# A delta-rule layer worked in pairs of heads: corrected queries as transposes, and the values' share in one bank

## The chip, the cores and the metric

The kernel runs on one core of a Trainium2 chip. The metric is the device time of one execution in microseconds (us). Engines are named as the profile names them: PE is TensorE's matmul stream and PEld its weight loads, DVE is VectorE, ACT is ScalarE, POOL is GpSimd and SP the queue that starts most DMAs. Each engine works through its instructions in the order in which they stand, so an instruction that waits holds up what is behind it on the same engine.

## The reference

A trunk of four layers on a sequence of 1024 tokens with 1024 features, in float32. Layers 0 and 3 mix tokens with a short convolution, layer 1 with a diagonal state-space model, layer 2 with the RWKV-7 delta rule. After each mixer come a gated embedding and a LayerNorm. The change lies in layer 2, whose core is a recurrence over time, one 64 x 64 state per head, 16 heads:

```python
def _rwkv_step(state, inp):
    r_t, w_t, k_t, v_t, kk_t, a_t = inp
    sa = jnp.einsum("bhvk,bhk->bhv", state, -kk_t)
    state = (state * w_t[:, :, None, :] + sa[..., None] * (kk_t * a_t)[:, :, None, :]
             + v_t[..., None] * k_t[:, :, None, :])
    out = jnp.einsum("bhvk,bhk->bhv", state, r_t)
    return state, out
```

The kernel does not step through time. It cuts the sequence into chunks of 64 tokens, solves the coupling inside a chunk with a triangular inverse, and carries the state from chunk to chunk.

## The kernel before

The sequence is worked in two halves of 512 tokens (h = 0, 1). In a half, each of eight units m is a block of 128 features, that is a pair of heads, with eight chunks. The chunks stand in pairs: w = 0 or 1 says which of a pair, and so which 64 of the 128 partitions a chunk's rows take. Of every unit the kernel does these things, each a generator that is pulled between the others:

- The projections `sp` (k and r of the next units, `mm3`, lines 326 to 328) are long products of 512 columns on PE. Each weight is split into a high and a low part, with three products per k-tile. They are the filling between everything else.
- `use_k` and `use_r` build the rows of keys and queries (`kb`, `ra`) and, by transposes, `ant`.
- `prep` multiplies `kb` with `ra` to scores `s` (line 1995), masks them on DVE into `sca` (line 1999), copies others into `scr` (ACT, line 2001), gathers the blocks `dg` and transposes them into `mi` (DVE, line 2012), multiplies the values `uv` with `sca` (`wps`, line 2021), copies that into the rows of `uv` (line 2025), and transposes `kb` into two tiles `kbt`.
- `tsolve` inverts the triangle on DVE in 11 steps.
- `join` completes the inverse `tt` (products `zp`, `tp`, lines 2090 and 2098) and applies it: to `ant`, giving `at` (line 2113), to `ant` again with the operands exchanged, giving `a2` (line 2119), which is the corrected part of the queries and is copied into `ra` (line 2124), and to `kbt` through `at`, giving `gt` (line 2134), copied into `gbd` (line 2138).
- `seq` forms `p` = inverse times values (line 2164), `pd` (line 2179), walks the eight chunks (`pd<-state,gbd` on PE, line 2185, and the state's update on DVE, line 2186), multiplies the queries with the states (line 2194) and adds the scores times values (line 2201) to the output.
- `tail` and `back` normalize and transpose the output.

A unit's `prep` is followed by the `join` of the unit before it, whose `seq` then runs beside the next unit's projections.

What sets the order: a scheduler takes the instructions by priority (`join`, `prep`, `seq` and `tsolve` are raised) and hands out buffers from pools as they come free; the order on each engine comes out of that. The pools that matter here are `aux`, two PSUM banks, through which all of these small products and transposes go, and `a1`, 16 tiles of 128 x 512. In the first half, eight of these 16 hold the low parts of the inputs of the k projection (`xs1`). Of each unit, `a1` holds one of the two `uv` and the two `scr` in both halves, and in the second half also `ant`, two `kbt`, `tt` and `at`. A tile of `a1` is free again when the last instruction that uses it is done: for `uv` and `scr` that is the last product of line 2201 in that unit's `seq`.

Of the kernel before, what the change touches and what calls it, by code (L numbers as in the profile page):

```python
# [8 lines left out]
F32 = mybir.dt.float32  # L9
# [6 lines left out]
P = 128  # L16
# [122 lines left out]
def setup_consts(S):  # L139
    nc, A = S.nc, S.A  # L140
    S.ident = S.const.tile([P, P], F32, tag="ident", name="ident")
    make_identity(nc, S.ident)
    S.mean_w = S.const.tile([P, P], F32, tag="mean_w", name="mean_w")
    nc.gpsimd.memset(S.mean_w, 1.0 / D)
# [1389 lines left out]
CH = 64  # L1534
# [394 lines left out]
def inner_setup(S, rg, T_):  # L1929
    nc = S.nc  # L1930
# [27 lines left out]
    def aux(nm):  # L1958
        return S.paux.tile([P, HT], F32, tag="aux", name=nm)
# [4 lines left out]
    zero = rg.tile([P, 2], F32, tag="zero", name="zero")  # L1964
    G.memset(zero, 0.0)
# [7 lines left out]
    def prep(m, h, R):  # L1973
# [42 lines left out]
        pss = [aux("wps"), aux("wps")]  # L2016
        for c in range(4):
            for hd in range(2):
                for w in range(2):
                    rb, rk = rows_b[w], rows_k[w]  # L2020
                    last = nc.tensor.matmul(pss[w][rb, c * P + hd * 64:c * P + hd * 64 + 64], sca[rk, w, c, hd, :],
                                            R.uv[w][rk, c, hd * 64:hd * 64 + 64], start=True, stop=True)
        for w in range(2):
            rb = rows_b[w]
            SC.copy(R.uv[w][rb].rearrange("p a b -> p (a b)"), pss[w][rb, :])
# [45 lines left out]
    def join(m, h, R):  # L2071
# [35 lines left out]
        with S.tc.issue_after(last.ins):  # L2107
# [7 lines left out]
            ps = [aux("a2"), aux("a2")]  # L2115
            for c2 in range(4):
                for hd in range(2):
                    for w in range(2):
                        nc.tensor.matmul(ps[w][heads[hd], c2 * CH:(c2 + 1) * CH], an[rows_b[w], c2, heads[hd]],
                                         tt[rows_b[w], 2 * c2 + hd, :], start=True, stop=True)  # L2120
        at = slot(S, ("a0", "a1")[h], "at").rearrange("p (c s) -> p c s", c=4)
        SC.copy(at.rearrange("p c s -> p (c s)"), pa)
        for w in range(2):
            SC.copy(r5[:, :, w, acol[w]], ps[w][:, 0:256].rearrange("p (c t) -> p c t", c=4))
# [11 lines left out]
        for w in range(2):  # L2136
            for hd in range(2):
                SC.copy(g5[heads[hd], :, w, heads[hd]], pg[w][heads[hd], 0:256].rearrange("p (c t) -> p c t", c=4))
        yield
# [3 lines left out]
    def seq(m, h, R, dST):  # L2143
# [13 lines left out]
        for ph in range(2):  # L2157
            p1 = S.pseq.tile([P, 2, 2, P], F32, tag="p1", name="p1", bufs=2)
            clear(p1[:, 0, 0, 0:2])
            for k in range(2):  # L2160
                for hd in range(2):
                    for w in range(2):
                        rb = rows_b[w]
                        nc.tensor.matmul(p1[rb, w, k, heads[hd]], R.tt[rb, 2 * (2 * ph + k) + hd, :],
                                         R.uv[w][rb, 2 * ph + k, heads[hd]], start=False, stop=False, skip_group_check=True)
# [127 lines left out]
```

## Time and profile before

| | us |
|---|---|
| median of 3 runs (lowest, highest) | 2805.72 (2804.64, 2808.44) |
| the profiled execution | 2808.62 |
| its span in the trace | 2806.6 |
| PE busy | 2709.2 (97%) |
| DVE busy | 1961.2 (70%) |
| ACT busy | 1215.7 (43%) |
| POOL busy | 649.2 (23%) |
| DMA queue 1, share of 16 engines | 38.9% |

The page of the profile gives busy times over the whole span. A stretch is read from the windows, a wait from the list of waits, and an order of events from the timeline. A small float32 product of this kernel leaves two matmul records in the trace, and a transpose leaves one. In the trace, layer 2's units run from about 1300 to about 2060 us.

### The profile page before, as it was taken

Reading aid. Unit: us, or ns where it says so; the run is one execution under the profiler, and the core shown is the slowest. Engines: PE = TensorE matmul, PEld = TensorE weight load, DVE = VectorE, ACT = ScalarE, POOL = GpSimd, SP = SyncE. Lnnn points to the kernel's source line nnn. Section 1 sums busy time; section 2 is a strip of 40 time slices with the busy share of each in tenths; the row PEclk is TensorE's granted clock in tenths of the full one; section 3 lists DMA queues with packets and bytes.
Section 4 is the critical chain, followed back from the end, with each engine's and each line's share of the span. In section 5 each row is a group of like instructions: output and inputs, shape, how many; then the busy total and the mean of one; then the engine's idle time right before and its main releaser. Section 6 shows DMA issues by size and latency. Waiting matters only on the chain.

```text
span 2806.6 us, 43661 instructions
## 1 busy us (share of the span) xinstructions
PE 2709.2 (97%) x16491; PEld 2171.2 (77%) x16491; DVE 1961.2 (70%) x3464; ACT 1215.7 (43%) x2147; POOL 649.2 (23%) x699
## 2 busy tenths in 40 slices
PE   8999999999999999999999889999999999999998
PEld 7877788777886888677787667777777877887887
DVE  6787765477657445897778766877756678877544
ACT  3333322242226223566566675666643343224332
POOL 0143421321115232202243200333332211111000
PEclk9999999999999999999999899999899999999999
DMA  5333321347785333464223245222334433324511
GB/s 170 99 98 98 88 83 57 89 139 207 212 240 165 98 99 88 139 222 139 72 80 102 74 153 175 73 87 74 105 117 142 132 120 106 102 71 133 171 64 38
DMA packets 463138, 331.22 MB, mean 118 GB/s; under 512 B 51496, under 2 KB 398928, under 8 KB 462928
## 3 DMA queue, kind: packets, MB, share of 16 engines
q1 hardware_dynamic: 462928, 328.43, 38.9%
q8 instruction: 130, 2.13, 0.3%
q14 instruction: 80, 0.66, 0.1%
HBM read 250.50 MB, written 77.33 MB: 117 GB/s over the span
## 4 chain that ended last, share of the span: by engine, by line
PE 75%; DVE 12%; issue 4%; ACT 4%; DMA 3%; POOL 1%; SPq 0%; DVEq 0%; ACTq 0%; POOLq 0%
PE op L327 4%; PE op L326 4%; PE op L328 4%; PE sp L327 3%; PE sp L326 3%; PE sp L328 3%; PE gp L328 3%; PE gp L327 3%; PE gp L326 3%; PE s L1995 2%; PE zp L326 2%; PE zp L327 2%; PE zp L328 2%; PE qa L507 2%; PE qa L506 2%
## 5 line engine op out<-in xcount | busy, mean ns | idle before, releaser
L298 ACT CAST wh<-wraw 128x1024 fp32r<-128x1024 f32 x255 | 267.3, 1049 | 527.1 <-PE gp L327 186.8
L299 DVE TENSOR_TENSOR wl<-wraw,wh 128x1024 fp32r<-128x1024 f32 x255 | 334.1, 1311 | 216.0 <-ACT wh L298 209.0
L905 POOL TENSOR_TENSOR ln_s<-ln_s,rp 128x512 f32<-128x512 f32 x42 | 60.4, 1438 | 208.6 <-DVE rp L901 208.5
L2062 DVE TENSOR_TENSOR tv<-ti,mi 128x128 f32<-128x128 f32 (+3 forms) x128 | 95.1, 743 | 2.2
L920 POOL TENSOR_TENSOR rp<-r_0h,r_0l 128x512 f32<-128x512 f32 x24 | 38.8, 1650 | 168.6 <-PE op L327 168.6
L328 PE MATMUL gp<-r_1h,wl 128*128 128x512 f32 x192 | 76.2, 397 | 0.4 <-DVE wl L299 0.4
L328 PE MATMUL gp<-r_0h,wl 128*128 128x512 f32 x192 | 76.5, 398 | 0.0
L326 PE MATMUL gp<-r_1h,wh 128*128 128x512 f32 x192 | 76.4, 398 | 0.0
L326 PE MATMUL gp<-r_0h,wh 128*128 128x512 f32 x192 | 76.0, 396 | 0.0
L327 PE MATMUL gp<-r_0l,wh 128*128 128x512 f32 x192 | 76.0, 396 | 0.0
L327 PE MATMUL gp<-r_1l,wh 128*128 128x512 f32 x192 | 75.3, 392 | 0.0
L1995 PE MATMUL s<-ra,kb 64*128 64x128 f32 x512 | 69.0, 295 | 2.2 <-ACT scr L2001 0.9
L1995 PEld LDWEIGHTS s<-ra,kb 64*128 64x128 f32 x512 | 58.2, 194 | 15.1 <-ACT scr L2001 5.2
L2186 DVE SCALAR_TENSOR_TENSOR state<-state,pc,pd 128x64 f32<-128x64 f32 x120 | 33.3, 278 | 42.9 <-PE pd L2185 41.6
L2170 ACT COPY uv<-p 64x256 f32<-64x256 f32 x128 | 46.9, 367 | 31.7 <-PE p L2194 26.2
L2185 PEld LDWEIGHTS pd<-state,gbd 128*128 128x128 f32 x240 | 42.5, 207 | 21.8 <-DVE state L2186 12.4
L327 PE MATMUL sp<-xs0l,wh 128*128 128x512 f32 x128 | 56.7, 443 | 1.9 <-DVE xs0l L195 1.9
L326 PE MATMUL sp<-xs3h,wh 128*128 128x512 f32 x128 | 52.6, 416 | 5.3 <-DVE sg L1663 5.3
L326 PE MATMUL sp<-xs0h,wh 128*128 128x512 f32 x128 | 56.6, 442 | 0.4 <-ACT xs0h L195 0.4
L2260 POOL TENSOR_TENSOR yt<-yt,bv 128x512 f32<-128x512 f32 x16 | 20.8, 1302 | 154.0 <-ACT yt L2259 110.5
L328 PE MATMUL sp<-xs0h,wl 128*128 128x512 f32 x128 | 55.7, 435 | 0.0
L195 ACT CAST r_0h<-r 128x512 fp32r<-128x512 f32 x32 | 19.9, 620 | 81.5 <-DVE r L406 39.4
(864 smaller groups left out, 8905.2 us busy)
## 6 DMA issues: line engine op xcount, KB each, us to landing
wraw<-in_conv_w_in_dram SPq DMA_DIRECT2D x84, 512.0 KB
wraw<-in_rwkv_w_rkvz_dram SPq DMA_DIRECT2D x64, 512.0 KB
wraw<-in_ple_gate_dram SPq DMA_DIRECT2D x56, 512.0 KB
wraw<-in_conv_w_out_dram SPq DMA_DIRECT2D x24, 512.0 KB
xt<-xd SPq DMA_DIRECT2D x48, 256.0 KB
wraw<-in_ssm_w_in_dram SPq DMA_DIRECT2D x21, 512.0 KB
xd<-rp SPq DMA_DIRECT2D x40, 256.0 KB
wraw<-in_rwkv_w_out_dram SPq DMA_DIRECT2D x16, 512.0 KB
```

What stands on the lines that cost most here:

```text
L298: nc.scalar.copy(wh, raw)
L299: nc.vector.tensor_tensor(wl, raw, f32(wh[:]), ALU.subtract)
L326: nc.tensor.matmul(ps, lh, xh, start=(n == 0), stop=False)
L327: nc.tensor.matmul(ps, lh, xl, start=False, stop=False)
L328: nc.tensor.matmul(ps, ll, xh, start=False, stop=(n == kt - 1))
L506: nc.tensor.matmul(ps, wh[:, k0 + k, :], xh, start=first and k == 0, stop=False, skip_group_check=True)
L507: nc.tensor.matmul(ps, wh[:, k0 + k, :], xl, start=False, stop=False, skip_group_check=True)
L905: nc.gpsimd.tensor_tensor(s, s, rs, ALU.add)
L1995: nc.tensor.matmul(pss[hd][:, c * P:(c + 1) * P], kb[rows, 2 * c + w, :], ra[rows, 2 * c + w, :], start=True, stop=True)
L2062: V.tensor_tensor(tv, ti[:, b:8, 4 * b:4 * b + 4].unsqueeze(2).to_broadcast([P, n, c, 4]), mi[:, 4 * b:4 * b + 4, 0:c].rearrange("p q c -> ...
L2170: SC.copy(R.uv[w][rows_b[w], 2 * ph:2 * ph + 2, :], p1s[ph][rows_b[w], w])
L2185: nc.tensor.matmul(col, R.g[:, c, :], sv[:, c, :], start=False, stop=True, skip_group_check=True)
```

## The change

Three edits.

1. In `join`, the second set of 16 products (`a2`, two banks) goes. Instead the tile `at`, once ACT has copied it, is turned by four transposes of 128 x 128 into one bank, and the two copies into `ra` read from there. These transposes and copies stand at the end of `join`, behind `gt` and its copies.
2. In `prep`, the 16 products of values and scores, which filled half of each of two banks, fill one bank. One copy of 128 x 512 moves it into a new tile `uvb` from the pool `a1`, where two copies of 64 x 512 moved it into the rows of the two `uv`. `seq` reads `uvb` in its first products.
3. The two columns of zeros with which `seq` clears its banks are written once among the constants at the program's start, ahead of the identity, and no longer in layer 2.

```diff
 def setup_consts(S):
+    S.zero = S.const.tile([P, 2], F32, tag="zero", name="zero")
+    nc.gpsimd.memset(S.zero, 0.0)
...
-        pss = [aux("wps"), aux("wps")]
+        pss = aux("wps")
...
-                    last = nc.tensor.matmul(pss[w][rb, c * P + hd * 64:c * P + hd * 64 + 64], sca[rk, w, c, hd, :],
+                    last = nc.tensor.matmul(pss[rb, c * P + hd * 64:c * P + hd * 64 + 64], sca[rk, w, c, hd, :],
                                             R.uv[w][rk, c, hd * 64:hd * 64 + 64], start=True, stop=True)
-        for w in range(2):
-            rb = rows_b[w]
-            SC.copy(R.uv[w][rb].rearrange("p a b -> p (a b)"), pss[w][rb, :])
+        R.uvb = slot(S, "a1", "uvb").rearrange("p (c s) -> p c s", c=4)
+        SC.copy(R.uvb.rearrange("p c s -> p (c s)"), pss)
...
-            ps = [aux("a2"), aux("a2")]
-            for c2 in range(4):
-                for hd in range(2):
-                    for w in range(2):
-                        nc.tensor.matmul(ps[w][heads[hd], c2 * CH:(c2 + 1) * CH], an[rows_b[w], c2, heads[hd]],
-                                         tt[rows_b[w], 2 * c2 + hd, :], start=True, stop=True)
         at = slot(S, ("a0", "a1")[h], "at").rearrange("p (c s) -> p c s", c=4)
         SC.copy(at.rearrange("p c s -> p (c s)"), pa)
-        for w in range(2):
-            SC.copy(r5[:, :, w, acol[w]], ps[w][:, 0:256].rearrange("p (c t) -> p c t", c=4))
         yield
...
+        ps = aux("a2")
+        for c2 in range(4):
+            nc.tensor.transpose(ps[:, c2 * P:(c2 + 1) * P], at[:, c2, :], S.ident)
+        p3 = ps.rearrange("p (c s) -> p c s", c=4)
+        for w in range(2):
+            SC.copy(r5[:, :, w, acol[w]], p3[:, :, acol[w]])
         yield
...
-                                         R.uv[w][rb, 2 * ph + k, heads[hd]], start=False, stop=False, skip_group_check=True)
+                                         R.uvb[rb, 2 * ph + k, heads[hd]], start=False, stop=False, skip_group_check=True)
```

The scheduler orders the program anew from the edits on; before layer 2's units and behind them the engines' orders are the same. PE in a `join` of the first half, before (`a_` is a bank of the second product, `p_` one of the two banks of inverse times values, `pss` belongs to the next unit's keys):

```order
L2113 MATMUL at<-ant,tt 64x64 x15
L2119 MATMUL a_12476<-tt,ant 64x64 x8
L2164 MATMUL p_12592<-uv,tt 64x64 x2
L2119 MATMUL a_12477<-tt,ant 64x64 x5
L2134 MATMUL gt<-kbt,at 64x64 x8
L2119 MATMUL a_12477<-tt,ant 64x64 x3
L2164 MATMUL p_12592<-uv,tt 64x64 x5
L2164 MATMUL p_12602<-uv,tt 64x64 x4
L2134 MATMUL gt<-kbt,at 64x64 x8
L2179 MATMUL pd<-uv,kbt 64x64 x2
```

The same place on PE in the changed kernel, where `a<-ident,at` are the four transposes:

```order
L2113 MATMUL at<-ant,tt 64x64 x15
L2162 MATMUL p_12549<-uvb,tt 64x64 x7
L2162 MATMUL p_12559<-uvb,tt 64x64 x4
L2126 MATMUL gt<-kbt,at 64x64 x16
L2177 MATMUL pd<-uv,kbt 64x64 x8
L2162 MATMUL p_12559<-uvb,tt 64x64 x3
L2133 MATMUL a_12470<-ident,at 128x128 x4
L330 MATMUL sp<-xs0h,wl 128x512
```

`gt` now stands in one piece, behind 11 products of `p`; the turned queries come last, with a projection directly behind them. The second place is PE in `prep` of the first half, before: `s_` are the four banks of scores of a unit, `p_12592<-uv,scr` and `p_12602` belong to the output of the unit before the last.

```order
L1995 MATMUL s_12835<-ra,kb 128x128 x4
L2185 MATMUL pd<-state,gbd_9913 128x64
L1995 MATMUL s_12858<-ra,kb 128x128 x4
L2185 MATMUL pd<-state,gbd_9913 128x64
L2201 MATMUL p_12592<-uv,scr 64x64 x3
L1995 MATMUL s_12859<-ra,kb 128x128 x4
L2201 MATMUL p_12592<-uv,scr 64x64
L2185 MATMUL pd<-state,gbd_9913 128x64
L2201 MATMUL p_12592<-uv,scr 64x64 x4
L327 MATMUL sp<-xs1l,wh 128x512
L2194 MATMUL p_12602<-sbd,ra 128x128 x4
```

And in the changed kernel (`p_12559<-uv,scr` are the last output products of that unit's `seq`; `s_12815` and `s_12816` are the third and fourth bank of scores):

```order
L2192 MATMUL p_12559<-sbd,ra 128x128 x4
L328 MATMUL sp<-xs1h,wh 128x512
L329 MATMUL sp<-xs1l,wh 128x512
L330 MATMUL sp<-xs1h,wl 128x512
L2151 MATMUL p_13035<-zero,ident 128x2
L328 MATMUL sp<-xs1h,wh 128x512
L329 MATMUL sp<-xs1l,wh 128x512
L2199 MATMUL p_12559<-uv,scr 64x64 x8
L330 MATMUL sp<-xs1h,wl 128x512
L328 MATMUL sp<-xs1h,wh 128x512
L1996 MATMUL s_12815<-ra,kb 128x128
L1996 MATMUL s_12816<-ra,kb 128x128
```

Before, all four banks of scores stand ahead of the last output products; now the third and fourth stand behind them. This is so in four units of the first half and in none of the second. Behind these scores the changed kernel has 12 projection products (16 in one of the four units), `wps` and the eight transposes of `kb` before the next `zp`.

## Rows read from the trace of the kernel before

**Rows 1.** The page: busy times, and the shares of the last chain.

```profile
PE 2709.2 (97%) x16491; PEld 2171.2 (77%) x16491; DVE 1961.2 (70%) x3464; ACT 1215.7 (43%) x2147; POOL 649.2 (23%) x699
...
PE 75%; DVE 12%; issue 4%; ACT 4%; DMA 3%; POOL 1%; SPq 0%; DVEq 0%; ACTq 0%; POOLq 0%
```

**Rows 2.** Windows: stretch, length; PE, PEld, DVE, ACT, POOL busy (instructions); PEclk, DMA share, GB/s.

```profile
1300.00:2060.00 760.00, 718.13 (x7368) 572.30 (x7367) 587.79 (x1234) 491.33 (x1049) 219.04 (x223) 0.94 0.33 101
...
1345.00:1545.00 200.00, 192.39 (x2375) 156.86 (x2375) 158.89 (x373) 131.81 (x304) 71.13 (x74) 0.95 0.29 88
```

**Rows 3.** PE's waits, 1290 to 2070 us (total, times, longest).

```profile
PE zp L2090 <- DVE t L2082: 6.5, 6, 3.0
...
PE pd L2185 <- DVE state L2186: 4.6, 6, 1.9
PE p L2201 <- ACT uv L2170: 4.1, 5, 1.5
PE gt L2134 <- ACT gbd L2138: 4.0, 13, 0.6
```

**Rows 4.** Timeline of PE in one join (start, duration, first to last end).

```profile
1457.88 0.93 PE L2113 MATMUL at<-ant,tt 64*64 64x64 f32 x26
...
1458.70 0.46 PE L2119 MATMUL a<-tt,ant 64*64 64x64 f32 x10
```

**Rows 5.** Timeline of PE around four transposes.

```profile
1449.79 0.39 PE L327 MATMUL sp<-xs0l,wh 128*128 128x512 f32 x1
1450.03 0.60 PE L2032 MATMUL kbtp<-ident,kb 128*128 128x128 f32 x4
1450.38 0.48 PE L328 MATMUL sp<-xs0h,wl 128*128 128x512 f32 x1
```

**Rows 6.** ACT's copies of lines 2122, 2138, 2025 (ns: min/median/max).

```profile
L2122 ACT COPY at<-at x16: 570/586/587, 1350.6 to 2048.6; 128x512 f32<-128x512 f32 x16
...
L2138 ACT COPY gbd<-gt x64: 361/367/370, 1352.6 to 2052.5; 64x256 f32<-64x256 f32 x64
...
L2025 ACT COPY uv<-wps x32: 564/582/588, 1312.5 to 2013.3; 64x512 f32<-64x512 f32 x32
```

**Rows 7.** Timeline from the last scores of a unit to `zp`.

```profile
1442.39 0.42 DVE L1999 TENSOR_TENSOR sca<-s,mask 128x256 f32<-128x256 f32 x1 [0.39 <-PE s L1995]
...
1442.85 0.82 ACT L2008 COPY dg<-sca 32x256 f32<-32x256 f32 x2 [0.43 <-DVE sca L1999]
...
1444.81 2.04 DVE L2012 STREAM_TRANSPOSE mi<-dg 128x1024 f32<-128x1024 f32 x1
...
1446.21 0.69 PE L2201 MATMUL p<-uv,scr 128*64 128x64 f32 x16
...
1446.98 0.65 ACT L2001 COPY scr<-s 128x256 f32<-128x256 f32 x2 [0.17 <-PE p L2201]
...
1447.92 1.15 PE L2021 MATMUL wps<-uv,sca 64*64 64x64 f32 x32
...
1451.58 1.12 DVE L2077 STREAM_TRANSPOSE tt<-ti 128x256 f32<-128x256 f32 x2
...
1452.56 0.40 DVE L2082 STREAM_TRANSPOSE t<-tt 128x256 f32<-128x256 f32 x1
...
1453.11 0.69 PE L2090 MATMUL zp<-t,m 32*32 32x32 f32 x32 [0.19 <-DVE t L2082]
```

**Rows 8.** Windows behind that join, and one near the start.

```profile
1460.00:1470.00 10.00, 9.79 (x124) 7.98 (x120) 6.81 (x17) 5.00 (x12) 3.88 (x4) 0.73 0.31 94
1470.00:1480.00 10.00, 10.00 (x81) 8.76 (x80) 8.47 (x23) 5.58 (x14) 1.42 (x3) 0.93 0.48 146
...
18.00:20.00 2.00, 2.00 (x6) 1.55 (x5) 1.41 (x2) 0.00 (x0) 0.00 (x0) 0.50 1.02 376
```

**Rows 9.** Timeline of PE at the program's start.

```profile
4.18 1.00 PE L211 MATMUL pxt<-ident,xraw 128*128 128x128 f32 x2 [4.18 <-DMA xraw<-in_x_dram]
...
8.05 6.26 PE L211 MATMUL pxt<-ident,xraw 128*128 128x128 f32 x29 [0.72 <-DMA xraw<-in_x_dram]
```

More of the change, by code (lines that the diff above doesn't have):

```diff
@@ L1962, in sq @@
         return S.pseq.tile([P, HT], F32, tag="sq", name=nm)
-    zero = rg.tile([P, 2], F32, tag="zero", name="zero")
-    G.memset(zero, 0.0)
+    zero = S.zero
     heads = [slice(hd * 64, hd * 64 + 64) for hd in range(2)]
```

## The prediction

> **What bounds the kernel now.** I read the page first: PE is busy for 97% of the span and has 75% of the chain that ended last; DVE has 12%, ACT 4% [rows 1]. Then the windows, because the change touches only layer 2's units: from 1300 to 2060 us PE is busy 718.1 of 760, and in the steady part of the first half 192.4 of 200 [rows 2]. So a unit is bound by PE's queue. DVE is busy 77% and ACT 65% there, which is not enough to set the end by throughput, but both release PE. The list of PE's waits shows where: `zp` on the end of DVE's solve 6.5 us, the chunk chain on the state 4.6, the output products on copied values 4.1, `gt` on the copies of `gbd` 4.0 [rows 3]. The reader is to see that no wait is long and that none stands for all units: PE has projections to do in between. Last, the granted clock: 0.94 over the 760 us [rows 2]. It has two levels, 2.4 and 1.2 GHz, so 0.94 means 12% of that time at the lower one, and 0.06 x 760 = 46 us of full-speed work not done.
>
> **The second product.** It goes in all 16 joins: 16 products each, 32 records. Two groups of such records, 26 in 0.93 us and 10 in 0.46 us, give (0.93 - 0.46) / 16 = 0.029 us for one more [rows 4], so 32 of them take 0.94 us. Four transposes take 0.35 us from their first start to the next product's start, and 0.60 to their own last end [rows 5]. A join so loses 0.59 us of PE by starts, 0.34 by ends. I take 0.50, nearer to the reading by starts, since the small products too are taken by starts. In the order of the change the last join of the first half has no projection beside it, so PE's time is not what counts there; 15 x 0.50 = 7.5 us off (bounds 5.1 and 8.8).
>
> **The waits of the join.** With two banks, before, the second half of `gt` had to wait until `gbd` was copied out: 4.0 us over 13 times [rows 3]. `gt` now stands in one piece, and this wait goes. Two come. `gt` needs the copy of `at`, 0.59 us [rows 6], with 11 products of `p` ahead of it, 22 x 0.029 = 0.64 us: I take 0.1 us per join for the hand-over. Behind `gt` are `pd`, the rest of `p` and the projections. The transposes need a bank, which comes free after two copies of `gbd`, 0.73 us [rows 6], covered by 8 products of `pd` and 3 of `p`, again 0.64 us: 0.15 us per join. Together 16 x 0.25 = 4.0, which is what went: 0, bounds -4 (full cover) and +4 (twice that). The copies into `ra` end later than before, but the first product that reads the queries stands only behind the chain's fifth step.
>
> **The values' share.** PE does the same 16 products. ACT does one copy in place of two of 0.58 us [rows 6], 9.3 us less over 16 units. ACT is busy 491 of 760 us [rows 2], so a third of its time is free and PE, not ACT, is the queue that is full: 0; if all of it were on the path it would be -9.3. The 16 products now write the two halves of one bank. If the halves had to take turns there, `wps` would take up to twice its 1.15 us [rows 7], 16 x 1.15 = 18 us more. The rows speak against it: `at` is written by two halves into one bank already, and its records are part of the 0.029 us above [rows 4]. The Trainium skill, "TensorEngine Tiling (Array Packing)", section "Gotcha 1: PSUM Pressure", says that different row tiles cannot use the same PSUM bank at the same time. By that rule the sum would end 18 us higher; the trace does not agree, as far as `at` shows it, and it is left as a rival with a small chance.
>
> **The zeros.** One tiny memset moves ahead of the identity. The first transpose waits for the input's DMA until 4.18 us [rows 9]: 0.
>
> **The tile `uvb`.** It is a fourth tile of `a1` per unit in the first half, where eight of 16 are taken. The last two score banks need `scr` tiles that come free with the last output products. Before, they were computed earlier and lay in the two banks until then: the copies waited for PE's output products to 1446.98 [rows 7]. Now the scores themselves stand behind these products in four units. From their end to `zp`, DVE and ACT need two masks at 0.42 us, `dg` 0.82, `mi` 2.04, `tt` 1.12, `t` 0.40 [rows 7]: 5.2 us, and hand-overs. PE has 12 projections at 0.24 us by starts [rows 5], `wps` 1.15 and eight transposes at 0.35 per four: 4.7 us. Before, PE waited 0.19 us here [rows 7]. I take 1 us per unit more, +4, and expect 3 of it back: projections that now stand inside the chunk chain cover some of the 8.7 us of waits there [rows 3]. Net +1, bounds -4 and +12 (3.0, the longest `zp` wait of the rows, in each of the four).
>
> **The sum.** -7.5 + 0 + 0 + 0 + 1 = -6.5 us. The profiled execution took 2808.6 us, 2.9 over the median of the runs; from it 2802.1, from the median 2799.2. I forecast 2799, with an own range of 2795 to 2802.
>
> **Rivals.**
>
> Clock, worse. Half clock follows joins: 0.73 and 0.93 in the two windows behind the one in the rows, 3.4 us of work lost in one fall [rows 8]. At the start 29 transposes in a row, then a pause, are followed by a window at 0.50 [rows 8, 9]. If transposes in place of products bring four more falls among 16 joins, +13.6 against -6.5 gives 2813: slower. The gain is gone from two more falls on (+6.8). Against it: four transposes last 0.35 us, and those of [rows 5] pass between projections of 0.39 and 0.48 us without a fall. The Trainium skill, "TensorE: Matmul & The Clock Gate", section "Part 4: PE-mode transpose", says that transposes do not count as PE work for the full clock; the trace's start agrees as far as it goes (0.50 after them).
>
> Clock, better. Projections now stand directly behind the turned queries, where there were only small products. Three falls fewer would be -10.2: 2789.
>
> `zp` waits. The solve's tail comes late in all four units by 3.0 us and none of it is given back: +12 - 7.5 = +4.5, 2810. For it: `zp`'s is the longest list of waits already. It decides where a unit's wait, less what comes back, is over 2 us.
>
> No gain. PE's shorter queue only waits longer for the state and the solve, as in the 42 us of 760 in which it is idle now: 2805. For it speaks that DVE's chain is 77% busy; against it, that idle time is spread thin.
>
> One bank costs: +18 - 6.5, 2817.
>
> **Chances.** My forecast 0.44, clock better 0.12, no gain 0.18, `zp` waits 0.11, clock worse 0.12, one bank 0.03. The range that holds 8 in 10 runs from 2788, a little under the better clock, to 2812, just short of the worse one. A measurement of this kernel can tell about 0.2%, 5.6 us, from no change, so faster means under 2800.1 and slower over 2811.3. Faster: the better clock and four fifths of the forecast, 0.47. Slower: the worse clock, one bank, a third of the `zp` case, 0.19. Same: the rest, 0.34.
>
> **What will show it.** Right: four records of `a<-ident,at` per join at about 0.35 us; PE's busy time from 1300 to 2060 down by 7 to 8 us; no wait of `gt` on `gbd`; `wps` at about 1.15 us in one bank. Waits of `zp` on `t` tell the slot case: over 10 us in total and it holds. PEclk over the units tells the clock: 0.94 for no change, under 0.93 or over 0.95 for a rival. I am wrong if the span changes by more than 3 us outside 1300 to 2060.

## The result, and the profile after

| | before, us | changed, us |
|---|---|---|
| median of 5 runs each (lowest, highest) | 2804.64 (2797.26, 2808.44) | 2790.42 (2786.80, 2792.86) |
| the profiled execution | 2808.62 | 2788.27 |
| its span | 2806.6 | 2786.4 |

The ratio is 0.995, 95% interval 0.9932 to 0.9969: the change is faster by 14.2 us. The forecast was 2799 in a range of 2788 to 2812. The side is right and the range holds the time, but the gain is about twice the one forecast (6.5), and the narrower range of the forecast alone, 2795 to 2802, does not hold it.

The page of the changed kernel: busy times, and the shares of the last chain.

```profile
PE 2681.5 (96%) x16043; PEld 2139.2 (77%) x16043; DVE 1962.9 (70%) x3464; ACT 1207.8 (43%) x2131; POOL 644.4 (23%) x699
...
PE 71%; DVE 15%; ACT 5%; issue 5%; DMA 3%; POOL 1%; SPq 0%; DVEq 0%; ACTq 0%; POOLq 0%
```

PE is busy for 27.7 us less than in [rows 1], at 448 records fewer: 16 joins lost 32 records each and got four. Its share of the chain fell, DVE's and ACT's rose.

The windows of the changed kernel (columns as in [rows 2]).

```profile
0.00:1300.00 1300.00, 1265.33 (x5898) 1009.70 (x5899) 878.48 (x1467) 465.53 (x698) 331.43 (x395) 0.99 0.45 134
1300.00:2060.00 760.00, 708.74 (x7015) 555.13 (x7015) 595.48 (x1253) 491.39 (x1049) 218.88 (x228) 0.94 0.33 102
2060.00:2786.40 726.40, 707.43 (x3134) 574.42 (x3132) 488.96 (x745) 250.91 (x384) 94.09 (x77) 0.99 0.36 110
1345.00:1545.00 200.00, 186.85 (x2215) 149.34 (x2214) 163.62 (x383) 133.44 (x305) 70.66 (x77) 0.94 0.31 95
```

From 1300 to 2060 us PE is busy 9.4 us less than in [rows 2], at the same granted clock of 0.94. This stretch is fixed while the units end earlier (their last `zp` starts at 2026.5 in place of 2044.0 us), so in the changed kernel it holds some 17 us of later work; what the change takes off PE is the 27.7 us of the whole span. The clock did not move, and what stands at half clock is looked at below.

PE's waits there, 1290 to 2070 us (total, times, longest).

```profile
PE zp L2090 <- DVE t L2082: 6.6, 6, 3.8
PE pd L2183 <- DVE state L2184: 5.9, 11, 1.8
PE zp L2090 <- DVE gn_s L1598: 4.7, 4, 1.4
PE a L2133 <- ACT gbd L2130: 3.5, 5, 1.4
PE s L1996 <- DVE kb L1741: 3.4, 5, 1.3
PE p L2199 <- ACT uv L2168: 2.7, 3, 1.5
```

Against [rows 3]: `gt` no longer waits for `gbd`; the transposes (`a`) wait for it instead, 3.5 us. The wait of `s` on `kb` grew, from 0.7 to 3.4. `zp` on `t` reads 6.6 as before, but the wait on `gn_s` has to be added to it, as the timeline of one of its four cases shows:

```profile
1377.83 0.39 DVE L2082 STREAM_TRANSPOSE t<-tt 128x256 f32<-128x256 f32 x1
1378.15 0.12 DVE L1598 TENSOR_TENSOR gn_s<-gn_s,rs_t 128x8 f32<-128x8 f32 x1
1378.37 0.69 PE L2090 MATMUL zp<-t,m 32*32 32x32 f32 x32 [1.42 <-DVE gn_s L1598]
```

`zp` reads `t`, which ends at 1378.22, and starts 0.15 us later; `gn_s`, the next instruction on DVE, ends 0.05 us behind `t`, and so the list names it. It is a wait for the solve like the others. All waits of `zp`, before and in the changed kernel (busy us, mean ns of one | idle before them and what ended it):

```profile
L2090 PE MATMUL zp<-t,m 32*32 32x32 f32 x512 | 11.1, 192 | 6.6 <-DVE t L2082 6.5
...
L2090 PE MATMUL zp<-t,m 32*32 32x32 f32 x512 | 11.5, 194 | 11.8 <-DVE t L2082 6.6 <-DVE gn_s L1598 4.7 <-DVE rs_t L1597 0.3
```

So `zp` waits 5.2 us more for the solve than before, and the prediction's sign for late scores, over 10 us in total, is met. In the four units with late scores it waits 1.4, 1.4, 1.4 and 0.3 us, 4.5 in all, where it waited 1.9 before. What that costs the experiments tell.

The timeline of PE in one join of the changed kernel (start, duration from the first start to the last end), which answers to [rows 4, 5].

```profile
1823.68 0.33 PE L2113 MATMUL at<-ant,tt 64*64 64x64 f32 x2
...
1824.08 1.03 PE L2113 MATMUL at<-ant,tt 64*64 64x64 f32 x29
1824.89 0.92 PE L2162 MATMUL p<-uvb,tt 64*64 64x64 f32 x22
1825.79 0.69 PE L2126 MATMUL gt<-kbt,at 64*64 64x64 f32 x32
1826.41 0.69 PE L2177 MATMUL pd<-uv,kbt 128*64 128x64 f32 x16
1827.03 0.44 PE L2162 MATMUL p<-uvb,tt 64*64 64x64 f32 x6
1827.40 0.65 PE L2133 MATMUL a<-ident,at 128*128 128x128 f32 x4
1827.81 0.48 PE L328 MATMUL sp<-xs1h,wh 128*128 128x512 f32 x1
```

From the first `at` to the projection behind the turned queries it is 4.13 us; the four transposes take 0.41 by starts and 0.65 to their own end. The 32 records of `gt` stand together and take 1826.41 - 1825.79 = 0.62 us, 0.019 each, where the forecast took 0.029 per record [rows 4].

What the small products of all 16 units take on PE, from 1300 to 2070 us, in the kernel before (busy us, mean ns of one | idle before them and what ended it; records that stand mixed count in both groups):

```profile
L2021 PE MATMUL wps<-uv,sca 64*64 64x64 f32 x512 | 29.9, 228 | 1.6 <-ACT scr L2001 1.6
L2119 PE MATMUL a<-tt,ant 64*64 64x64 f32 x512 | 29.1, 236 | 1.8 <-ACT at L2122 0.4
...
L2134 PE MATMUL gt<-kbt,at 64*64 64x64 f32 x512 | 22.4, 230 | 4.0 <-ACT gbd L2138 4.0
```

The same groups in the changed kernel:

```profile
L2022 PE MATMUL wps<-uv,sca 64*64 64x64 f32 x512 | 23.7, 235 | 2.5 <-DVE sca L2000 2.0 <-ACT scr L2002 0.3
L2126 PE MATMUL gt<-kbt,at 64*64 64x64 f32 x512 | 13.0, 241 | 0.7 <-ACT at L2116 0.3
L2133 PE MATMUL a<-ident,at 128*128 128x128 f32 x64 | 10.7, 286 | 3.6 <-ACT gbd L2130 3.5
```

The second product went from 29.1 to 10.7. But `gt` and `wps`, of which not one product went, fell too, by 9.4 and 6.2, at equal time of one record. They are busy for less because more of them run side by side: that is the reading on which the rest turns. The three falls add up to 34 us, more than PE's 27.7, because records that stand mixed count twice and other groups rose, for one the transposes `kbtp` of `kb`, from 18.2 to 21.8.

The values' share in one bank, on PE's timeline:

```profile
1372.54 1.22 PE L2022 MATMUL wps<-uv,sca 64*64 64x64 f32 x32 [0.15 <-ACT scr L2002]
1373.69 0.51 PE L328 MATMUL sp<-xs1h,wh 128*128 128x512 f32 x1
```

In the kernel before, the two banks of the first unit went one after the other, 16 records in 1.14 us each:

```profile
1309.70 1.14 PE L2021 MATMUL wps<-uv,sca 64*64 64x64 f32 x16
1310.77 0.50 PE L328 MATMUL sp<-xs1h,wl 128*128 128x512 f32 x1
1311.23 1.14 PE L2021 MATMUL wps<-uv,sca 64*64 64x64 f32 x16
```

Not all units before were like this: the one in [rows 7] had both banks free. And the copy behind the one bank, which answers to [rows 6] (ns: min/median/max):

```profile
L2025 ACT COPY uvb<-wps x16: 567/585/589, 1310.3 to 1998.3; 128x512 f32<-128x512 f32 x16
```

The 32 records written by two row halves into one bank last 1.22 us, against 1.15 in two banks in [rows 7], and one copy of 128 x 512 costs what each of the two copies of 64 x 512 cost. So two row halves in one bank cost at most 0.07 us, in 16 units about 1 us and not 18: that rival is out. The Trainium skill, "TensorEngine Tiling (Array Packing)", section "Gotcha 1: PSUM Pressure", says that different row tiles can't use the same bank at the same time; the trace does not agree, for two row halves that write different partitions of the bank.

### The profile page after: what moved, and what is told of

Read it like the earlier page. It is cut to its first block, busy times and chain, and to the rows that moved or that the text cites. A ratio compares the mean times of both kernels' runs of the same rounds, so it can differ in the third digit from the quotient of the medians.

```text
span 2786.4 us, 42742 instructions
## 1 busy us (share of the span) xinstructions
PE 2681.5 (96%) x16043; PEld 2139.2 (77%) x16043; DVE 1962.9 (70%) x3464; ACT 1207.8 (43%) x2131; POOL 644.4 (23%) x699
## 4 chain that ended last, share of the span: by engine, by line
PE 71%; DVE 15%; ACT 5%; issue 5%; DMA 3%; POOL 1%; SPq 0%; DVEq 0%; ACTq 0%; POOLq 0%
PE op L328 4%; PE op L330 4%; PE op L329 4%; PE gp L330 3%; PE gp L329 3%; PE gp L328 3%; PE sp L328 3%; PE sp L329 2%; PE sp L330 2%; PE s L1996 2%; PE qa L508 2%; PE qa L509 2%; PE qa L510 2%; DVE wl L301 2%; PE zp L328 2%
## 5 line engine op out<-in xcount | busy, mean ns | idle before, releaser
L2168 ACT COPY uv<-p 64x256 f32<-64x256 f32 x128 | 46.9, 366 | 29.7 <-PE p L2192 27.7
L330 PE MATMUL sp<-xs0h,wl 128*128 128x512 f32 x128 | 55.8, 436 | 0.0
L328 PE MATMUL sp<-xs1h,wh 128*128 128x512 f32 x128 | 53.9, 421 | 0.0
```

The source lines that it names most:

```text
L328: nc.tensor.matmul(ps, lh, xh, start=(n == 0), stop=False)
L330: nc.tensor.matmul(ps, ll, xh, start=False, stop=(n == kt - 1))
L2168: SC.copy(R.uv[w][rows_b[w], 2 * ph:2 * ph + 2, :], p1s[ph][rows_b[w], w])
```

## How a run's time is split below

Runs of one kernel differ by up to 0.9% (2792.82 to 2817.11 for before, beside the first experiments), more than the edits are worth, and what differs is mostly TensorE's clock. So each run's span is split by its own record of the mean granted clock, which is given for every run. For the changed kernel's profile that record is:

```profile
core 0: 2786.4 us, clock 0.978
```

2786.4 x 0.978 = 2725 us is the span without what the lower level cost (called the full-speed part: PE's work, and its idle time), and 2786.4 x 0.022 = 61 us is called half clock. Summed from windows of 4 us, half clock is 61.0 in this profile and 66.6 in that of before, whose full-speed part is 2806.6 - 66.6 = 2740.0.

The parts vary very differently. In 65 runs of the kernel before that were timed beside the experiments, half clock lay between 39 and 76 us, and the span went with it (correlation 0.89, 0.58 us of span per us of half clock: some of it falls where PE would have waited). The mean of the full-speed part of before is known to about 1 us.

The full-speed part alone is not a fair comparison of kernels that differ in half clock. Within a kernel the span moves by 0.58 us per us of half clock and not by 1, so taking all of it off flatters the kernel that had more, by 0.42 us for each. The zeros alone show it: an edit that gave no time has a full-speed part 3.5 us lower, at 4.6 us more half clock. The last column therefore gives the mean span against that of before at equal half clock: the difference of the spans less 0.58 times the difference in half clock, with errors from the scatter of all runs about that slope. Where the two measures differ, it is the better one. For the zeros it still shows 1.6 us, so a difference of about 2 us says little. The means, with two standard errors:

| kernel (runs) | median, us | ratio to before | full-speed part | half clock | at equal half clock |
|---|---|---|---|---|---|
| before (65, in three sets) | 2801.72, 2804.22, 2801.84 | 1 | 2742.5 ± 1.0 | 58.2 ± 1.9 | 0 |
| zeros alone (12) | 2804.83 | 1.0001 [0.9988, 1.0015] | 2739.0 ± 2.9 | 62.8 ± 4.5 | -1.6 ± 1.4 |
| turn alone (12) | 2802.50 | 0.9999 [0.9981, 1.0018] | 2734.2 ± 2.1 | 66.5 ± 5.6 | -4.8 ± 1.4 |
| one bank alone (12) | 2803.02 | 0.9998 [0.9987, 1.001] | 2740.2 ± 2.2 | 61.2 ± 3.3 | -1.1 ± 1.4 |
| values' share alone (12) | 2797.68 | 0.9979 [0.9963, 0.9995] | 2733.4 ± 1.9 | 62.2 ± 4.2 | -7.4 ± 1.4 |
| change, second product late (8) | 2791.12 | 0.9955 [0.9937, 0.9973] | 2732.9 ± 2.7 | 55.8 ± 3.5 | -10.7 ± 1.6 |
| one bank, second product late (6) | 2784.83 | 0.9937 [0.9916, 0.9957] | 2731.9 ± 3.0 | 52.0 ± 6.9 | -13.3 ± 1.9 |
| change without `uvb` (6) | 2780.42 | 0.9921 [0.9899, 0.9942] | 2728.7 ± 2.0 | 50.5 ± 4.0 | -17.1 ± 1.9 |
| change (5 and 6) | 2790.42, 2787.98 | 0.995 [0.9932, 0.9969], 0.9947 [0.993, 0.9964] | 2727.0 ± 1.5 | 60.3 ± 2.3 | -14.6 ± 1.4 |
| change, turn early (12) | 2802.03 | 1.0 [0.9985, 1.0014] | 2741.1 ± 1.6 | 59.8 ± 3.3 | -0.8 ± 1.4 |
| change, no turn (6) | 2779.68 | 0.9917 [0.9902, 0.9932] | 2717.7 ± 2.7 | 60.2 ± 4.7 | -24.0 ± 1.9 |

## The experiments

The first four runs had three theories. A: the join is the cause, its block of products became shorter. B: the values' share is the cause, which had been put at nothing. C: the edits are worth the forecast's 6.5 us, and the rest is half clock that falls elsewhere in the new order. P and F come with the ninth run.

**The turn alone.** The kernel before without the 16 products and their copies ahead of `gt`, and with the transposes and theirs behind the copies of `gbd`, as in the change:

```diff
-            ps = [aux("a2"), aux("a2")]
...
+        ps = aux("a2")
+        for c2 in range(4):
+            nc.tensor.transpose(ps[:, c2 * P:(c2 + 1) * P], at[:, c2, :], S.ident)
...
```

> The kernel before with the transposes alone (two banks and two copies for the values' share, zeros in layer 2). Theory A, the join's block: from the first product of at to the last of the block PE took about 5.9 us before and about 4.4 after at full clock; the transposes bring all of that, in 16 joins. It expects 10 to 17 us under the kernel before, and blocks of 4.4 us. Theory B, the values' share (one copy less on ACT, one bank less) brings half or more: 3 to 7 us under. Theory C, the order and the half clock fall out differently in every program and the edits themselves are worth 6.5 us: between 0 and 13 us under, with the difference in the half-clock time.

2802.50: no change in time, so A as the whole cause falls. The full-speed part is 8.3 ± 2.3 us lower than before's, close to the forecast's 6.5 to 7.5, and half clock 8.3 ± 5.9 higher; the two cancelled. At equal half clock it is 4.8 ± 1.4 us under before. In the profile the block of a join fell from 5.9 to 4.4 us where nothing interrupts it, 16 times 1.5 = 24 us. `gt` in the units took 12.3 us and the transposes 10.5, so both parts of the join are as in the change, and `wps`, still in two banks, took 33.2. PE's work at full speed fell by 19 (2642.6 to 2623.5) but its idle time rose by 12 (97.4 to 109.0). More than half of that rise stands in one place, from `zp` of the sixth unit of the first half to that of the eighth. The window of this kernel there (columns as in [rows 2]):

```profile
1533.10:1610.80 77.70, 62.64 (x740) 49.26 (x740) 71.59 (x149) 54.29 (x117) 20.86 (x24) 0.93 0.32 87
```

The same stretch in the changed kernel:

```profile
1519.80:1598.90 79.10, 72.57 (x732) 57.05 (x732) 64.89 (x143) 50.42 (x110) 17.54 (x22) 0.81 0.28 83
```

PE idles 15.1 us here with the turn alone, 6.5 in the change, and 8.6 in the kernel before. PE's longest waits in the first of these windows, the turn alone:

```profile
PE pd L2183 <- DVE state L2184: 3.4, 2, 1.9
PE zp L2090 <- DVE rs_t L1593: 2.6, 1, 2.6
PE sp L327 <- DVE xs3l L195: 2.3, 2, 1.6
PE s L1995 <- ACT scr L2001: 2.3, 1, 2.3
```

And in the second, the change:

```profile
PE p L2192 <- ACT sbd L2188: 1.3, 3, 0.8
PE p L2199 <- ACT uv L2168: 1.2, 2, 0.8
PE pd L2183 <- DVE state L2184: 0.9, 3, 0.4
```

The waits on the state (3.4 to 0.9), on the solve (`zp`, under `rs_t`), on `xs3l` and on `scr` (2.3 to 0.4) are what the change is without. Projections are not lacking in either: 96 records of `sp` start in the first window and 84 in the second. Why the one order waits more than the other is not shown. The same windows show the other side: the granted clock is 0.81 in the change where it idles less, against 0.93, and the stretch is 1.4 us longer in the change (79.1 against 77.7). In these two profiles half clock takes back here all that the shorter waits save.

**The values' share alone.** The change with the second product as before, 16 products into two banks ahead of `gt`:

```diff
-            nc.tensor.transpose(ps[:, c2 * P:(c2 + 1) * P], at[:, c2, :], S.ident)
+                        nc.tensor.matmul(ps[w][heads[hd], c2 * CH:(c2 + 1) * CH], an[rows_b[w], c2, heads[hd]],
+                                         tt[rows_b[w], 2 * c2 + hd, :], start=True, stop=True)
...
```

> The change without the transposes: the second product stays, the values' share goes to one bank, one copy and the tile uvb, zeros among the constants. Theory A expects -1 to +5 us against the kernel before: blocks stay at 5.9 us, the third and fourth score bank stand behind the last output products in the first half, and zp waits for t longer than the 6.5 us of before. Theory B expects 7 us under or more.

2797.68, 4.0 us under the runs of before beside it, which is under A's range and short of B's 7. The full-speed part is 9.1 ± 2.1 us below before's, and at equal half clock it is 7.4 ± 1.4: by these B holds, for about half of the change. `wps` took 22.9 us in these units, `gt` 24.3 and the second product 30.3: the saving in the values' products is there without the turn, and that in `gt` is not. Added to the turn's part it makes 17.4 at full speed, where the change has 15.5 ± 1.8, and 12.2 at equal half clock, where the change has 14.6 ± 1.4.

**The second product, late.** The change with the 16 products in place of the transposes, behind the copies of `gbd`:

```diff
-        ps = aux("a2")
+        ps = [aux("a2"), aux("a2")]
...
-            nc.tensor.transpose(ps[:, c2 * P:(c2 + 1) * P], at[:, c2, :], S.ident)
...
+                    nc.tensor.matmul(ps[w][heads[hd], c2 * CH:(c2 + 1) * CH], an[rows_b[w], c2, heads[hd]],
+                                     tt[rows_b[w], 2 * c2 + hd, :], start=True, stop=True)
...
```

> The change with the second product in place of the transposes at the same late place: gt in one piece, no wait of gt on gbd, but 32 records where there are 4. Theory A in two parts: if the gain of the block is the smaller number of columns, this kernel is 8 to 10 us slower than the change; if a part of it is gt in one piece, it is still 4 to 8 us under the kernel before, with blocks of about 5.0 us. Theory C expects no order in it.

2791.12. The full-speed part is 5.9 ± 3.1 above the change, 0.37 us per join (3.9 ± 2.1 and 0.24 at equal half clock), which is the price of the form alone at one place. That is under the 8 to 10 us expected if the columns alone counted; that a part of the gain is `gt` in one piece holds. The late product took 21.4 us on PE, against 29.1 at its old place, and `gt` 12.1: the place alone sets both together in one piece each. Half clock is 4.5 lower here, so the two medians are alike.

**The change without `uvb`.** One bank, and two copies back into `uv` as before:

```diff
-        R.uvb = slot(S, "a1", "uvb").rearrange("p (c s) -> p c s", c=4)
-        SC.copy(R.uvb.rearrange("p c s -> p (c s)"), pss)
+        for w in range(2):
+            rb = rows_b[w]
+            SC.copy(R.uv[w][rb].rearrange("p a b -> p (a b)"), pss[rb, :])
...
```

> The change with one bank for the values' share but two copies back into the rows of uv, so no fourth tile in a1. Theory A expects the scores before the last output products again, fewer waits of zp (under 6 us in all), and 0 to 5 us under the change. Theory B (one copy, 9.3 us of ACT) expects 3 to 9 us over the change.

2780.42, the fastest kernel that computes the reference: 21 us under the runs of before beside it, and 7.6 to 10 under the change: more than A's 0 to 5, and against B. The scores stand ahead of the last output products again, and in the four units in which the change has them late `zp` now comes about 1 us or more behind `t` and waits for nothing. All waits of `zp` are 9.8 us here, not under 6 as A expected. The full-speed part is that of the change (+1.7 ± 2.5), and half clock is lower by 9.8 ± 4.6; at equal half clock this version is 2.5 ± 2.3 us under the change. So `uvb` with its late scores costs about 2 us, if anything, and the rest of the 7.6 to 10 is half clock. That the order brings the lower half clock is not shown.

**One bank alone.** The kernel before with one edit:

```diff
-        pss = [aux("wps"), aux("wps")]
+        pss = aux("wps")
...
-            SC.copy(R.uv[w][rb].rearrange("p a b -> p (a b)"), pss[w][rb, :])
+            SC.copy(R.uv[w][rb].rearrange("p a b -> p (a b)"), pss[rb, :])
```

> The kernel before with one part of the change: the 16 products of the values' share write the two halves of one bank, and two copies of 64x512 bring them back into uv as before. The second product stays, uvb and the zeros are not there. Theory B (the gain comes from the bank that the values' share no longer takes; the turn by itself gave nothing, 2802.5): 2780 to 2787, near the kernel with one bank, no uvb and the turn (2780.4), and blocks of the join still 5.9 us. Theory A2 (both parts are needed: the turn's 1.5 us per join pay only once the second bank is free): 2793 to 2798, a third of the way from 2801.7 to 2780.4. Theory C (what decides is where the half-clock stretches fall in the new order): no value is favoured, but the time net of clock would be that of before less 2 at most, and the work lost to half clock in units would differ from 44 us by what the span differs.

2803.02; full speed 2.3 ± 2.4 lower, and 1.1 ± 1.4 at equal half clock. The bank by itself is nothing that can be told from zero, so the strong form of B falls, and A2's 2793 to 2798 with it. `wps` fell to 21.6 us and PE's work by 8.6 (2642.6 to 2634.0), but idle rose by 11.8 (97.4 to 109.2): a saving that only came sooner to the next wait. The largest rise is at the transposes of `kb` behind `wps`: they wait 4.5 us for POOL to finish `kb`, where before they never waited. With the turn beside it the bank is worth 5.5 ± 2.9 at full speed (turn alone against the change without `uvb`), and 12.3 ± 2.3 at equal half clock; the two kernels are 16 us of half clock apart, so the size is uncertain.

**One bank, second product late.** As the one before, with the 16 products and their copies moved behind the copies of `gbd`:

```diff
         pg = [aux("gt"), aux("gt")]
...
+        ps = [aux("a2"), aux("a2")]
...
+                    nc.tensor.matmul(ps[w][heads[hd], c2 * CH:(c2 + 1) * CH], an[rows_b[w], c2, heads[hd]],
+                                     tt[rows_b[w], 2 * c2 + hd, :], start=True, stop=True)
```

> As the one before, and the second product of 16 stands where the change puts the transposes, behind the copies of gbd. With uvb the late product gave the same time as the transposes (2791.1 against 2790.4), at a block 0.7 us longer. If the place is what counts and not the form, this gives 2778 to 2783, like the kernel with the transposes, one bank and no uvb (2780.4). If the form counts (the late product holds two auxiliary banks at once, the transposes one), 2785 to 2792.

2784.83, at the edge between the two forecasts. Moving the product is worth 8.3 ± 3.7 at full speed beside one bank (12.1 ± 2.2 at equal half clock); with `uvb` (values' share alone against the second product late) it was worth 0.5 ± 3.3 (3.3 ± 2.0). The one copy into `uvb` and the later place therefore don't add up; why they don't, the runs don't tell.

**The zeros alone.**

```diff
-    zero = rg.tile([P, 2], F32, tag="zero", name="zero")
-    G.memset(zero, 0.0)
+    zero = S.zero
```

> The kernel before with the zeros among the constants alone. All theories: 2801.7, within 3 us. If it comes out 5 or more to either side, then a kernel's time varies by that much without any reason in the units, and differences of this size between the other runs say nothing.

2804.83, ratio 1.0001: nothing, as forecast. It also shows what two equal orders of PE's units look like: half clock in the units was 47.8 us in this profile, 44.3 in that of before. The places differ more than the sums: near the end of the second half the granted clock is 0.76 over 36 us before (1984 to 2020 us), and 1.00 over the same work here (1980 to 2016).

**The change once more**, unedited.

> The changed kernel once more, for its profile. Time 2790.4, within 3. Theory C in its strict form (the program sets where TensorE falls to half clock): the stretches in units start within 6 us of 1342, 1380, 1454, 1536, 1592, 1626, 1738, 1778, 1932, 1970, 1988 us, and the work lost in units is 44 us again. In its loose form (they fall by chance within a kernel): other places, and a loss that differs by over 4 us, with a span that differs by about as much.

2787.98 us. From the third unit on half clock falls at the same places as in the first profile, and each time in the same amount to 1.7 us (11.9 and 10.2 us at 1536 to 1540, 6.8 twice at 1592, 3.4 twice at 1626 and at 1738, 5.1 twice at 1988); in the first two units it was 11.9 in place of 6.8, and in all units 49.5 in place of the 44 expected. So in this kernel most places come again. Before and the zeros alone, whose orders are equal too, agree less; how far the order sets the places stays open.

**The turn, early.** The change with the transposes and their copies right behind the copy of `at`, and no longer behind those of `gbd`:

```diff
         SC.copy(at.rearrange("p c s -> p (c s)"), pa)
+        ps = aux("a2")
+        for c2 in range(4):
+            nc.tensor.transpose(ps[:, c2 * P:(c2 + 1) * P], at[:, c2, :], S.ident)
...
```

> The change with one edit: the four transposes and their two copies stand right behind the copy of at, ahead of gt, where the product of 16 stood before. Bookkeeping used from here on: span = work of PE at full speed (busy less what half clock adds) + idle of PE + half clock; before 2642.6 + 97.4 + 66.6, the change 2620.5 + 104.9 + 61.0 (again 2619.9 + 104.4 + 63.1). Theory P (the place decides: gt in one piece, without a wait for a bank, is most of the work saved): with the turn early gt breaks in two again, the work rises by 8 to 16 to 2628 to 2636, and the time to 2795 to 2800. Theory F (the form decides, four transposes into one bank in place of 16 products into two): work 2618 to 2624, as in the change; the time then differs from 2788 to 2790 only by half clock, within 6.

2802.03: all of the gain is gone, also that of the values' share. The full-speed part is 14.1 ± 2.2 above the change (13.8 ± 1.8 at equal half clock). The work in the profile is 2627.7, just under P's numbers and above F's, idle is 109.5 against 104.9, and the time is 2 us over P's. P holds in the main and F falls. PE's timeline in a join shows why:

```profile
1879.40 0.86 PE L2162 MATMUL p<-uvb,tt 64*64 64x64 f32 x21
1880.24 0.33 PE L2119 MATMUL a<-ident,at 128*128 128x128 f32 x1
1880.49 0.68 PE L2132 MATMUL gt<-kbt,at 64*64 64x64 f32 x16
1881.11 0.55 PE L2119 MATMUL a<-ident,at 128*128 128x128 f32 x3
1881.58 0.56 PE L2177 MATMUL pd<-uv,kbt 128*64 128x64 f32 x10
1882.07 0.68 PE L2132 MATMUL gt<-kbt,at 64*64 64x64 f32 x16
1882.69 0.45 PE L2177 MATMUL pd<-uv,kbt 128*64 128x64 f32 x6
1883.06 0.44 PE L2162 MATMUL p<-uvb,tt 64*64 64x64 f32 x6
1883.43 1.05 PE L1719 MATMUL pss<-c_ones,sq 128*128 128x2 f32 x8
```

The turn holds one of the two banks while `gt` wants both. `gt` so breaks in two again, by bank, which is by chunk of the pair: 16 records in 1881.11 - 1880.49 = 0.62 us, and 16 in 1882.69 - 1882.07 = 0.62. In one piece, as in the change, the two chunks alternate, and all 32 take 0.62. A chunk's rows are one half of the 128 partitions, so a piece for one bank gives the other row half of the array no work. From the first `at`, at 1878.06, to the end of this block it is 5.4 us, against 4.1.

**The change without a turn.**

```diff
-        ps = aux("a2")
-        for c2 in range(4):
-            nc.tensor.transpose(ps[:, c2 * P:(c2 + 1) * P], at[:, c2, :], S.ident)
-        p3 = ps.rearrange("p (c s) -> p c s", c=4)
-        for w in range(2):
-            SC.copy(r5[:, :, w, acol[w]], p3[:, :, acol[w]])
```

> The change without the corrected queries: neither product nor transposes, nor their copies into ra (so the queries stay uncorrected and the output is not the reference's). It bounds the price of the turn. Forecast's price of four transposes, 0.35 to 0.60 us, 16 times: work 5.6 to 9.6 below the change, 2611 to 2615. If PE is the bound throughout, the span less half clock falls by as much, 2725 to 2717. Rival (join waits come in its place): work falls, idle rises by half of that or more, and the span less half clock stays within 3 of 2725. Time without a change in half clock: 2779 to 2784, or 2786 to 2790.

2779.68. The full-speed part is 9.3 ± 3.1 lower (9.4 ± 2.2 at equal half clock): 0.58 us per join, the price of four transposes where they stand. In the one profile the work fell by 16 us, more than expected, to 2604, and idle rose by 3. The rival of join waits in their place did not hold. The second product, late, comes to (2732.9 - 2717.7) / 16 = 0.95 us per join (0.83 at equal half clock). The forecast had 0.94 for the product and 0.35 to 0.60 for the transposes; the reading to the transposes' own end was the right one.

**Second profiles.** Two kernels unedited, one run each.

> The kernel with one bank and the second product late, for a second profile: its half clock was the least of all, 29.0 us in the units and 44.3 in all. If the order of a kernel's instructions sets the sum (the change gave 61.0 and 63.1 in two profiles, before and the zeros alone 66.6 and 64.6), 41 to 48 in all. If it falls by chance in each run, it moves towards the mean of the others, 52 or more, and its span to 2787 or more.

> The kernel before with the transposes alone, for a second profile. It was 2732.5 without half clock, 6.5 below the mean of before and the zeros alone (2740.0, 2738.1), and its half clock 70.3, the most of all. Order sets it: half clock 67 to 74, rest 2731 to 2734. Chance: half clock under 64, and a span under 2798.

The record of the first, one bank with the late product:

```profile
core 0: 2779.0 us, clock 0.983
```

That of the second, the turn alone:

```profile
core 0: 2788.5 us, clock 0.982
```

The first repeats its low half clock (47.0 us by windows of 4 us, 44.3 before). The second does not repeat its high one: 50.0 in place of 70.3, with a span 14.3 us shorter and idle time in the same place again (14.4 us from the sixth to the eighth `zp`). Its full-speed part is 2738.5, not the 2731 to 2734 of the first expectation: with 20 us less half clock the rest rose by 6, where the slope of 0.58 gives 8 or 9. So a single profile can't say that a kernel is at half clock more than another; the means of the table can, to a few microseconds.

## Why the prediction was right, and where it was not

- The range. That it holds 2790.42 is in part luck: its lower end, 2788, stood there for the better clock, which did not come. The gain came from a term that was put at 0.
- The second product. Forecast 7.5 us off (5.1 to 8.8) with the join's waits at nothing. Measured at full speed: 8.3 ± 2.3 alone, 6.4 ± 2.4 on top of the values' share, 5.9 ± 3.1 for the form at one place; at equal half clock 4.8 ± 1.4, 7.2 ± 1.8 and 3.9 ± 2.1. The net is about right, but it came out of two terms that were both too small. PE saved more, 19 us with the turn alone, since the pieces of `gt` came together; and PE's idle time, which I had cancel, rose by 12: the waits of `zp` on the solve from 6.6 to 13.5 and those of the chunk chain on the state from 4.6 to 9.0 above all.
- The values' share. This is the step that failed: "PE does the same 16 products", costed at 0, with ACT's copies as the only gain. It measured 9.1 ± 2.1 us alone, and 7.2 ± 2.6 on top of the turn (7.4 ± 1.4 and 9.7 ± 1.9 at equal half clock). The products are the same, but their order is not: with two banks they went in pieces by bank in many units, one chunk at a time, and took 28.8 to 33.2 us in the four profiles with two banks; in one bank the two chunks alternate, and they took 21.6 to 23.7 in every other. I had read the price from one unit in which both banks happened to be free, 1.15 us [rows 7], and 16 times that is 18.4, not 29.9. ACT's single copy is not shown to be the gain: beside the turn, the version with two copies is no slower at full speed (1.7 ± 2.5 from the change), and at equal half clock it is the faster one. That the saving on PE is what the share gains in time is argued and not shown, since one bank alone, with the same saving on PE, was worth only 2.3 ± 2.4 (1.1 ± 1.4), and `uvb` with it 6.8 ± 2.9 more (6.3 ± 1.8). A part is seen in the wait of the transposes of `kb` for POOL, 4.5 us with one bank alone; the rest is open.
- `uvb`. Forecast +1 (-4 to +12): 4 us of waits of `zp` in four units, and 3 of them given back. Without `uvb` these waits are gone, 4.5 us in the change against none, so the mechanism came as forecast; the price is -1.7 ± 2.5 at full speed and 2.5 ± 2.3 at equal half clock. The rival's 12 us did not come. Its sign, over 10 us of waits, can't tell it: `zp` waits 11.8 us in the change, and 13.5 with the turn alone, where there is no `uvb`.
- One bank written by two row halves: 1.22 us against 1.15. Out.
- The zeros: nothing, as forecast.
- No gain. This rival is true in part: of the 22 us that PE's full-speed work fell (2642.6 to 2620.5), 7.5 came back as idle time; with one bank alone all of the saving did.
- The clock. Forecast no change. Half clock is 60.3 ± 2.3 against 58.2 ± 1.9 before: neither rival came. The Trainium skill, "TensorE: Matmul & The Clock Gate", section "Part 4: PE-mode transpose", says that transposes don't count as work for the full clock. With 64 transposes in place of 256 products no effect of that size is seen here; leaving out the turn altogether did not change half clock either (60.2 ± 4.7).
- The sum. Full speed -15.5 ± 1.8 in place of -6.5, half clock +2.1 ± 3.0 in place of 0; at equal half clock -14.6 ± 1.4. The median moved by 14.2. The failed term alone, 0 in place of -7 to -10, makes up the difference.
- The signs. PE's busy time from 1300 to 2060 us fell by 9.4, near the 7 to 8 named, but this number is not what the change takes off PE, as said above. Nothing changed outside the units, as the prediction required: PE's busy time to 1300 us is 1265.3 against 1265.5, and from the start of the last `zp` to the end it is 759.9 us against 762.6.

## What to carry to other kernels

Small products that use one half of the array each are cheap when the halves alternate, so count in how many pieces they stand, over all units and not in one: a step that asks for two buffers of a small pool can get them one after the other, and its products then go by halves. Put such a step's output into one buffer, or place it where both are free: against the 16 products, the same four transposes gained about 7 us behind the copies of `gbd` and lost about 7 ahead of `gt`, where they held a buffer that `gt` wanted. A saving on the busiest engine is not yet time: with one bank alone all of it came back as waits. Where a record of the granted clock exists for every run, compare kernels at equal half clock: the turn's 5 us looked like none, and taking off all of half clock made them 8. And where the list of waits names a releaser that the instruction does not read, look in the timeline for what it does read.

## What the runs showed of the hardware that was not expected

One piece of 32 records of `gt`, on four quarters of the array in turn, took the 0.62 us that 16 records on two quarters take. The Trainium skill, "TensorEngine Tiling (Array Packing)", section "Key Properties", says that tiles operate independently and can run in parallel; the trace agrees, with 0.019 us per record against 0.039. Where all 16 records of a piece are on one quarter, as in a bank of `wps` before, they take 1310.77 - 1309.70 = 1.07 us to the start of the next product, 0.067 each.

In the change's two profiles half clock falls at the same places from the third unit on. The largest such stretch begins at the end of the chunk chain of the sixth unit; from 1533.2 to 1552.3 us no projection stands on PE (windows, columns as in [rows 2]):

```profile
1536.00:1540.00 4.00, 2.98 (x27) 2.34 (x26) 3.69 (x10) 1.76 (x5) 0.12 (x1) 0.69 0.30 89
1540.00:1548.00 8.00, 7.80 (x41) 6.58 (x42) 1.69 (x5) 3.86 (x10) 1.42 (x2) 0.50 0.61 170
```

PE waits in short pieces for a quarter of the first window, and in the next it is busy 97% of the time at 0.50, the lower of the two levels. Eight records of `s` take 2.07 us there (at 1543.49), and 1.16 at the higher level (at 1299.52).
